# Grouped-query attention: exponentials in place in PSUM, sums divided out early, low parts split on GpSimd

## The chip, the cores and the metric

The kernel runs on one core of one Trainium2 chip. Its time is the device time of one execution in microseconds (us). Five engines work side by side, each through its own instructions in order: TensorE (PE in the profile, with weight loads as PEld), VectorE (DVE), ScalarE (ACT), GpSimd (POOL) and SyncE (SP), which issues most of the DMAs. Matrix products land in PSUM, which has eight banks of 512 fp32 columns; the rest lives in SBUF.

## The reference

Two layers of a trunk with two parallel token mixers. 512 latent tokens and 256 context tokens of width 1024 go through one input projection; branch A is a neighbourhood attention with 8 heads of 64, branch B a grouped-query attention with 8 query heads over 2 key heads, in which latent queries read all 768 keys:

```python
def _attend(q, k, v):
    s = jnp.einsum('bqkgd,btkd->bkgqt', q, k).astype(jnp.float32) * (HEAD_DIM ** -0.5)
    p = jax.nn.softmax(s, axis=-1).astype(v.dtype)
    return jnp.einsum('bkgqt,btkd->bqkgd', p, v)

def _merge(a_att, b_att, a_z, b_z, g_a, g_b, w_o_a, w_o_b, w_out):
    o_a = (a_att * jax.nn.silu(a_z)) @ w_o_a
    o_b = (b_att * jax.nn.silu(b_z)) @ w_o_b
    merged = jax.nn.sigmoid(g_a) * o_a + jax.nn.sigmoid(g_b) * o_b
    return merged @ w_out
```

Context queries read context keys alone, and only layer 0 computes them, since the context of the last layer is not returned. The output is the latent stream.

## The kernel before, in words

Every fp32 product is made of low-precision products: an operand is split into a high part (a cast) and a low part (the operand less its high part), and PE runs high x high, high x low and low x high (`mm3`, L431). Weights are split as they arrive, in `load_w` and `load_w2` (L395, L410): DMA into `raw`, ACT casts to `whi` (L403, L418), and DVE or POOL subtracts to `wlo` (L406, L420). Which of the two is chosen by a small function per load: `pool_lo`, `mix_lo` (every other one on DVE), `bq_lo` (L424 to L426).

A layer goes through five stages: projections for branch A, neighbourhood attention, projections for branch B, grouped-query attention, and the merge with the output projection. Each stage opens its own PSUM tiles (`open_ps`, L103). The bank "f" and the two banks "t" stay open for the whole kernel; a stage adds "s" (scores), "v" (values) or "x" (more accumulators).

The grouped-query stage (L1114 to L1176) runs `pipeline` (L997) over eight heads. For head h it computes the scores, then the values of head h-1, and between them pieces of a list of fill work: gate projections (`g_chunks`, L642) and the first output projection (`o_chunks("a", ...)`, L662), each piece a product over all channels into bank "f", taken out by ACT (L614) or DVE (L692).

One head of 512 latent queries has four blocks of 128 queries by 768 keys (`gq_scores`, L1122). PE writes a block's scores into an "s" tile of two banks (L861, L862); two such tiles exist. DVE finds the row maximum (L1131, which also writes a scratch copy into `p`), ACT writes the exponentials into `p` in SBUF with their sums (L1132), ACT casts them to fp16 `h` (L802), and DVE (blocks 0, 2) or POOL (blocks 1, 3) subtracts for the low part (L803). A transposing DMA on SP's queue turns both parts into `ht` (L804), from which PE makes the values (L1148, L1149). The sums are divided out at the end of a head: `divide` (L806) takes reciprocals, PE spreads each column over partitions by a transpose (L811, four per head and two for its context part), and DVE multiplies them into the gate `zb` (L812). `head_out` (L789) adds the two halves of the value product and multiplies `zb`. In layer 0 each head also has a context part of 2 x 128 queries by 256 keys (`ctx_scores`, `ctx_values`) that goes the same way.

`stage_q` (L849) makes a head's query tile: ACT casts, DVE subtracts (L855). `prepare` (L679) splits the result of branch A, `za`, into `gah` and `gal` (ACT L656, POOL L657) before the first output projection.

The order on each engine isn't that of the text: a scheduler places the instructions when the kernel is built, by its own estimate of durations and of when tiles come free; `behind` pins some to their place. SP's queue, in order, holds weight loads, gate loads and the transposing DMAs together; a weight load waits there until one of three `raw` tiles is free.

Of the kernel before, what the change touches and what calls it, by code (L numbers as in the profile page):

```python
# [27 lines left out]
NP_GQ = (2, 4)  # L28
NH_GQ = (3, 4)
NT_NA = 2  # L30
P_LOG = 9.7
V_UP = 2.0 ** 14
NA_POOL = (1, 3)
SPLIT_POOL = (1, 3)
# [36 lines left out]
def hybrid_kernel(es: ExitStack, tc, x, ctx, cvec, w_ada, w_ada0, small, gvec, w_in, w_o_a, w_o_b, w_out,  # L71
# [28 lines left out]
    ps_pool(es, "t", 2, 512)  # L100
    es.callback(lambda: pm["es"].close())

    def open_ps(x=0, **kinds):  # L103
# [4 lines left out]
        pm["n"], pm["i"], pm["v_for"] = x + 1, 0, ()  # L108
        if x:
            kinds["x"] = (x, 512)  # L110
# [3 lines left out]
    def psw(n=512, kind="w"):  # L114
        if kind == "w":
            kind = "f" if pm["i"] % pm["n"] == 0 else "x"
            pm["i"] += 1
            if pm["i"] in pm["v_for"]:
                kind = "v"
# [464 lines left out]
    def layer(l, hx, nxt, start):  # L584
# [77 lines left out]
        def o_chunks(br, prepare, evac):  # L662
# [96 lines left out]
        if True:  # L759
# [29 lines left out]
            def head_out(po, e, dst, eng=None):  # L789
# [5 lines left out]
                S.copy(a, po[o:o + 64, :n])  # L795
                V.tensor_tensor(a, po[m:m + 64, :n], a, ALU.add)
                (eng or G).tensor_tensor(dst, dst, a, ALU.mult)

            def turned(p, n, out, eng):

                h = att["p"].tile([128, 2, n], F16, tag="h", name=nm("h"), bufs=att["nh"])
                S.copy(h[:, 0], p[:, :n])  # L802
                eng.tensor_tensor(h[:, 1], p[:, :n], h[:, 0], ALU.subtract)  # L803
                nc.sync.dma_start_transpose(out, h.rearrange("p a n -> p (a n)"))  # L804

            def divide(ps, r, e, dst, back):  # L806

                n = r.shape[-1]
                V.reciprocal(r, r)
                for i in range(n):  # L810
                    T.transpose(ps[:, 128 * i:128 * i + 128], r[:, i:i + 1].to_broadcast([128, 128]), ident)  # L811
                V.scalar_tensor_tensor(dst, ps[64 * e:64 * e + 64, :128 * n], back[64 * e:64 * e + 64], dst,  # L812
                                       ALU.mult, ALU.mult)

            def shrink(v, s, mx, row):
# [10 lines left out]
                V.tensor_scalar(s[:, 1:2], s[:, 1:2], 0.5, None, ALU.mult)  # L826
# [22 lines left out]
            def stage_q(src, e):  # L849
# [5 lines left out]
                V.tensor_tensor(rows(qs, 1 - e), q, F(rows(qs, e)), ALU.subtract)  # L855
# [11 lines left out]
            def ctx_scores(q, kh, kl, ct=None):  # L867
# [7 lines left out]
                if ct is not None:  # L875
                    V.tensor_scalar(mx, mx, P_LOG, None, ALU.add)
                p = p_tile()
# [4 lines left out]
                if ct is not None:  # L882
                    turned(p, 512, ct.rearrange("p a i k n -> p (a i k) n"), G)
# [616 lines left out]
```

## Time and profile before

| | |
|---|---|
| median of 3 runs (range) | 1127.67 us (1126.69 to 1128.68) |
| profiled execution | 1127.56 us, its span 1125.6 us |
| mean granted TensorE clock | 0.993 |
| busy PE / PEld / DVE / ACT / POOL | 1093.3 / 905.3 / 774.7 / 579.0 / 490.6 us |
| score blocks of the grouped-query stages | first exponential at 384.5 us, last at 1045.0 us |

Rows of groups name the line, engine, operation, output<-input tiles, shapes and count, then busy time and mean duration, then the engine's idle time before them and what ended it. A row of waits says who waited for whom: total us, times, longest. A row of the timeline begins with start and duration in us. A row of stages gives start and end, length, busy time of each engine with its instruction count, the granted TensorE clock as a share, the DMA share and GB/s. A row of one line's listing gives count and minimum/median/maximum in ns, then first and last start.

### The profile page before, as it was taken

How to read it: one execution, taken by the hardware profiler on the slowest of the kernel's cores; microseconds unless marked ns; L12 is line 12 of the kernel's file. 1: busy time of each engine (PE TensorE's matmuls, PEld its weight loads, DVE VectorE, ACT ScalarE, POOL GpSimd, SP SyncE). 2: the span in 40 equal slices, each digit the busy share in tenths (PEclk: the TensorE clock that was granted, in tenths of full speed). 3: DMA queues.
4: the chain of work that ended last, by engine and by line, in shares of the span. 5: the costliest groups of instructions: out<-in, count | busy, mean ns of one | idle time of the engine just before them, and what ended most of it. 6: DMA issues, size and time to landing. Idle time of an engine off the chain costs nothing.

```text
span 1125.6 us, 16862 instructions
## 1 busy us (share of the span) xinstructions
PE 1093.3 (97%) x5826; PEld 905.3 (80%) x5826; DVE 774.7 (69%) x1492; ACT 579.0 (51%) x1154; POOL 490.6 (44%) x405
## 2 busy tenths in 40 slices
PE   8999999999999999979999999999999999999998
PEld 5688888888998877757788888888888987776677
DVE  4666788897466477776577785458878765677473
ACT  6453266665433576755330284326666446776431
POOL 1054254654247144454521545235554563563531
PEclk9999999999999999989999999999999999999999
DMA  9454322242351488869633532553333236989742
GB/s 373 143 172 140 114 63 66 73 136 89 93 168 38 123 201 185 185 172 269 173 108 125 183 129 72 142 174 92 100 107 116 59 105 172 188 224 239 197 145 80
DMA packets 192222, 161.29 MB, mean 143 GB/s; under 512 B 116364, under 2 KB 158088, under 8 KB 190472
## 3 DMA queue, kind: packets, MB, share of 16 engines
q1 hardware_dynamic: 184800, 145.82, 46.8%
q0 software_dynamic: 2368, 7.87, 2.1%
q10 hardware_dynamic: 4968, 6.53, 1.7%
q8 instruction: 46, 0.75, 0.3%
q14 instruction: 40, 0.33, 0.1%
HBM read 115.58 MB, written 17.32 MB: 118 GB/s over the span
## 4 chain that ended last, share of the span: by engine, by line
PE 38%; issue 4%; DVE 3%; DMA 3%; POOL 2%; ACT 1%; SPq 1%; POOLq 0%; ACTq 0%
PE psx L435 6%; PE psx L433 6%; PE psx L434 6%; PE psf L433 4%; PE psf L434 4%; PE psf L435 4%; PE pss L955 1%; PE pss L861 1%; POOL wlo L406 1%; PE pss L862 1%; PE pst L779 1%; PE pst L1148 1%; DMA raw<-in_w_o_a_dram 1%; PE pst L1149 1%; DMA raw<-in_w_in_dram 1%
## 5 line engine op out<-in xcount | busy, mean ns | idle before, releaser
L420 POOL TENSOR_TENSOR wlo<-raw,whi 128x512 fp32r<-128x512 f32 x70 | 97.9, 1405 | 106.1 <-ACT whi L418 70.4
L433 PE MATMUL psf<-hx,whi 128*128 128x512 f32 (+1 forms) x360 | 138.0, 383 | 3.2 <-ACT zt L614 2.4
L435 PE MATMUL psf<-hx,wlo 128*128 128x512 f32 (+1 forms) x360 | 135.8, 377 | 0.0
L434 PE MATMUL psf<-hx,whi 128*128 128x512 f32 (+1 forms) x360 | 135.1, 375 | 0.0
L433 PE MATMUL psx<-whi,hx 128*128 128x512 f32 (+1 forms) x328 | 120.8, 372 | 0.0
L434 PE MATMUL psx<-wlo,hx 128*128 128x512 f32 (+1 forms) x328 | 119.6, 366 | 0.0
L435 PE MATMUL psx<-whi,hx 128*128 128x512 f32 (+1 forms) x328 | 119.5, 365 | 0.0
L418 ACT CAST whi<-raw 128x512 fp32r<-128x512 f32 x136 | 82.3, 620 | 64.0 <-DMA raw<-in_w_in_dram 35.3
L406 POOL TENSOR_TENSOR wlo<-raw,whi 128x512 fp32r<-128x512 f32 x40 | 61.2, 1535 | 122.1 <-ACT whi L403 80.1
L803 POOL TENSOR_TENSOR h<-p,h 128x768 f16<-128x768 f32 (+1 forms) x40 | 65.7, 1644 | 96.4 <-ACT h L802 72.0
L403 ACT CAST whi<-raw 128x512 fp32r<-128x512 f32 x88 | 54.1, 623 | 99.2 <-PE psx L435 34.2
L420 DVE TENSOR_TENSOR wlo<-raw,whi 128x512 fp32r<-128x512 f32 x66 | 73.6, 1115 | 30.6 <-ACT whi L418 29.0
L504 POOL TENSOR_TENSOR ss<-ss,ehalf 128x8 f32<-128x8 f32 (+2 forms) x40 | 62.5, 1566 | 72.9 <-DVE ss L501 72.8
L433 PEld LDWEIGHTS psf<-hx,whi 128*128 128x128 f32 x360 | 67.9, 188 | 15.4 <-ACT zt L614 3.7
L435 PEld LDWEIGHTS psf<-hx,wlo 128*128 128x128 f32 x360 | 67.8, 188 | 11.6
L1131 DVE CUSTOM_DVE_ANT_0 p<-pss,vb 128x768 f32<-128x768 f32 x64 | 60.3, 953 | 23.6 <-PE pss L862 21.1
L434 PEld LDWEIGHTS psf<-hx,whi 128*128 128x128 f32 x360 | 67.9, 189 | 10.3
L1132 ACT ACTIVATE p<-pss,mx 128x768 f32<-128x768 f32 x64 | 57.6, 900 | 34.7 <-DVE mx L1131 33.7
L435 PEld LDWEIGHTS psx<-whi,hx 128*128 128x128 f32 x328 | 61.9, 189 | 10.0
L434 PEld LDWEIGHTS psx<-wlo,hx 128*128 128x128 f32 x328 | 62.0, 189 | 9.2
L433 PEld LDWEIGHTS psx<-whi,hx 128*128 128x128 f32 x328 | 61.8, 189 | 8.9
L435 PE MATMUL psx<-hx,wlo 128*128 128x256 f32 (+1 forms) x208 | 68.0, 327 | 0.0
(362 smaller groups left out, 3095.8 us busy)
## 6 DMA issues: line engine op xcount, KB each, us to landing
raw<-in_w_in_dram SPq DMA_DIRECT2D x168, 256.0 KB, 2.9
rawb<-in_w_ada_dram SPq DMA_DIRECT2D x48, 256.0 KB, 2.8
raw<-in_w_out_dram SPq DMA_DIRECT2D x32, 256.0 KB, 2.9
tg<-gs SPq DMA_DIRECT2D x4, 1536.0 KB, 6.8
rawx<-in_w_ada_dram SPq DMA_DIRECT2D x4, 1024.0 KB, 9.8
rawy<-in_w_ada_dram SPq DMA_DIRECT2D x4, 1024.0 KB, 9.5
gs<-zt ACTq DMA_DIRECT2D x16, 256.0 KB, 2.0
raw<-in_w_o_a_dram SPq DMA_DIRECT2D x16, 256.0 KB, 3.4
```

The source lines that it names most:

```text
L403: S.copy(hi[:, :n], raw[:, :n])
L406: e.tensor_tensor(lo[:, :n], raw[:, :n], F(hi[:, :n]), ALU.subtract)
L418: S.copy(hi, raw)
L420: lo_eng(i).tensor_tensor(lo, raw, F(hi), ALU.subtract)
L433: T.matmul(ps, lhs[0], rhs[0], start=first, stop=False)
L434: T.matmul(ps, lhs[0], rhs[1], start=False, stop=False)
L435: T.matmul(ps, lhs[1], rhs[0], start=False, stop=last)
L504: G.tensor_tensor(ss, ss, ehalf[:, :n], ALU.pow)
L779: T.transpose(pt[:, c0:c0 + 128], src, ident)
L803: eng.tensor_tensor(h[:, 1], p[:, :n], h[:, 0], ALU.subtract)
L1131: V.tensor_tensor_reduce(p, pss, lift, -1.0, 3e38, ALU.add, ALU.min, mx[:, 0:1])
L1132: S.activation(p, pss, AF.Exp, bias=mx[:, 0:1], accum_out=r[:, i:i + 1])
```

## The change

It rewrites the grouped-query stage and what feeds it, in both layers.

- The tiles "s" become two of three banks (1536 columns). `gq_scores` takes two blocks at a time: one row maximum over both, then two exponentials written over the scores, in PSUM. The SBUF tiles `p` are gone there, and with them the constant `P_LOG`.
- `turned` divides first: per block a reciprocal of the sum and a scaling by 2^14 (one column each, DVE), then ACT's cast from PSUM with that scale, then on DVE one instruction that scales and subtracts. POOL no longer takes part. `divide` is removed; `head_out` takes the scale back with the values' own factor.
- The context part of layer 0 does the same, and is put behind the fill work (`rest` in `values_of`).
- "t" is opened per stage: two banks as before, but one in the grouped-query stage, where "v" is gone.
- Low parts that move to POOL: those of all gate weights (`g_chunks`), of the weights of the first output projection, and of the grouped-query queries.

```diff
-NP_GQ = (2, 4)
-NH_GQ = (3, 4)
+NH_GQ = (5, 6)
-P_LOG = 9.7
+P_UP = 2.0 ** 14
...
-    ps_pool(es, "t", 2, 512)
-    def open_ps(x=0, **kinds):
+    def open_ps(x=0, t=2, **kinds):
...
+        kinds["t"] = (t, 512)
...
-            return fill_chunks(col0, None, gs[c], False, mix_lo)
+            return fill_chunks(col0, None, gs[c], False, pool_lo)
...
-                    st["w"] = load_w2(src, 256 * i, 4, pool_lo if br == "b" and i == 0 else mix_lo)
+                    st["w"] = load_w2(src, 256 * i, 4, pool_lo if br == "a" or i == 0 else mix_lo)
...
-                S.copy(a, po[o:o + 64, :n])
-                V.tensor_tensor(a, po[m:m + 64, :n], a, ALU.add)
+                if back is None:
+                    S.copy(a, po[o:o + 64, :n])
+                    V.tensor_tensor(a, po[m:m + 64, :n], a, ALU.add)
+                else:
+                    S.activation(a, po[o:o + 64, :n], AF.Copy, scale=back[o:o + 64])
+                    V.scalar_tensor_tensor(a, po[m:m + 64, :n], back[m:m + 64], a, ALU.mult, ALU.add)
                 (eng or G).tensor_tensor(dst, dst, a, ALU.mult)
...
-            def turned(p, n, out, eng):
+            def turned(p, r, cuts, out):
+                n = cuts[-1][1]
                 h = att["p"].tile([128, 2, n], F16, tag="h", name=nm("h"), bufs=att["nh"])
-                S.copy(h[:, 0], p[:, :n])
-                eng.tensor_tensor(h[:, 1], p[:, :n], h[:, 0], ALU.subtract)
+                for i, (c0, c1) in enumerate(cuts):
+                    V.reciprocal(r[:, i:i + 1], r[:, i:i + 1])
+                    V.tensor_scalar(r[:, i:i + 1], r[:, i:i + 1], P_UP, None, ALU.mult)
+                    S.activation(h[:, 0, c0:c1], p[:, c0:c1], AF.Copy, scale=r[:, i:i + 1])
+                    V.scalar_tensor_tensor(h[:, 1, c0:c1], p[:, c0:c1], r[:, i:i + 1], h[:, 0, c0:c1],
+                                           ALU.mult, ALU.subtract)
                 nc.sync.dma_start_transpose(out, h.rearrange("p a n -> p (a n)"))
...
-                V.tensor_tensor(rows(qs, 1 - e), q, F(rows(qs, e)), ALU.subtract)
+                eng.tensor_tensor(rows(qs, 1 - e), q, F(rows(qs, e)), ALU.subtract)
...
-                if ct is not None:
-                    V.tensor_scalar(mx, mx, P_LOG, None, ALU.add)
-                p = p_tile()
+                p = p_tile() if ct is None else pss
...
-                    ps = psw(512, "v")
-                    po = ps[:, 0:256]
-                    divide(ps[:, 256:512], r, e, dst, back)
+                    po = psw(256, "t")
...
-            gq_es = open_att(f"gq{l}", 768, NP_GQ[l], NH_GQ[l])
-            open_ps(s=(2, 1024), v=(1, 512))
+            gq_es = open_att(f"gq{l}", 768, 0, NH_GQ[l])
+            open_ps(t=1, s=(2, 1536))
...
-                for i in range(4):
-                    pss = ps_score(768)
-                    scores(pss, q[:, 128 * i:128 * i + 128], kh, kl,
+                for j in range(2):
+                    ps = ps_score(1536)
+                    scores(ps, q[:, 256 * j:256 * j + 128], kh, kl,
                            [(0, 512, cut(0, 512)), (512, 256, cut(512, 768))])
-                    p = p_tile()
+                    scores(ps, q[:, 256 * j + 128:256 * j + 256], kh, kl,
+                           [(768, 256, cut(0, 256)), (1024, 512, cut(256, 768))])
                     mx = sp.tile([128, 2], F32, tag="mx", name=nm("mx"), bufs=8)
-                    V.tensor_tensor_reduce(p, pss, lift, -1.0, 3e38, ALU.add, ALU.min, mx[:, 0:1])
-                    S.activation(p, pss, AF.Exp, bias=mx[:, 0:1], accum_out=r[:, i:i + 1])
-                    turned(p, 768, ht[:, i], G if i in SPLIT_POOL else V)
-                    run(att["bg"], 1)
-                return ht, r
+                    V.tensor_reduce(mx, ps.rearrange("p (i n) -> p i n", i=2), AX, ALU.max, negate=True)
+                    r = sp.tile([128, 2], F32, tag="r", name=nm("r"), bufs=8)
+                    for i in range(2):
+                        p = ps[:, 768 * i:768 * i + 768]
+                        S.activation(p, p, AF.Exp, bias=mx[:, i:i + 1], accum_out=r[:, i:i + 1])
+                    for i in range(2):
+                        turned(ps[:, 768 * i:768 * i + 768], r[:, i:i + 1], [(0, 768)], ht[:, 2 * j + i])
+                        run(att["bg"], 1)
+                return ht
...
-                divide(psw(512, "t"), r, e, dst, vs[:, 1:2])
...
-                q = stage_q(qbv[:, h // 2, :], h % 2)
+                q = stage_q(qbv[:, h // 2, :], h % 2, G)
```

More of the change, by code (lines that the diff above doesn't have):

```diff
@@ L787, in transpose_split, with head_out @@
                 return hi, lo
-            def head_out(po, e, dst, eng=None):
+            def head_out(po, e, dst, eng=None, back=None):
                 n = dst.shape[-1]
@@ L825, in shrink @@
                 V.reciprocal(s[:, 0:1], s[:, 1:2])
-                V.tensor_scalar(s[:, 1:2], s[:, 1:2], 0.5, None, ALU.mult)
+                V.tensor_scalar(s[:, 1:2], s[:, 1:2], 0.5 / P_UP, None, ALU.mult)
             def rows(a, half):
```

53 lines of the change are left out of this document (23 added, 30 removed).

## The prediction

> **What bounds the kernel now.** I read the page's busy shares first, then stages chosen by what runs in them, then waits, then time around the worst wait. In this table of stages each row gives the stretch, its length, and for PE, PEld, DVE, ACT and POOL the busy time.
>
> ```profile
> span 1125.6 us, 16862 instructions
> PE 1093.3 (97%) x5826; PEld 905.3 (80%) x5826; DVE 774.7 (69%) x1492; ACT 579.0 (51%) x1154; POOL 490.6 (44%) x405
> 0.00:380.00 380.00, 375.96 (x2161) 318.33 (x2162) 260.46 (x573) 192.91 (x406) 157.31 (x142) 1.00 0.39 127
> 380.00:580.00 200.00, 184.81 (x1030) 149.70 (x1029) 136.01 (x237) 112.72 (x218) 87.38 (x62) 0.97 0.75 185
> 580.00:935.00 355.00, 352.98 (x1793) 297.44 (x1793) 259.64 (x500) 172.68 (x354) 165.43 (x150) 1.00 0.38 117
> 935.00:1075.00 140.00, 134.86 (x630) 102.34 (x629) 92.79 (x146) 92.02 (x164) 68.62 (x47) 1.00 0.87 205
> ```
>
> PE sets the time nearly everywhere: outside the two grouped-query stages it idles 4.0 us before 380 and 2.0 us between 580 and 935. The stages that the change rewrites, 380 to 580 (layer 0) and 935 to 1075 (layer 1), hold 15.2 + 5.1 = 20.3 us of PE idle, so both PE work and PE waits are worth time there. The next rows are PE's waits in 380 to 560, then the execution around the longest, then busy time and granted clock (third figure from the end) in 5 us pieces.
>
> ```profile
> PE psv L811 <- DVE ho L796: 5.8, 1, 5.8
> ...
> PE pss L861 <- ACT p L880: 1.3, 1, 1.3
> PE pss L861 <- ACT p L1132: 0.9, 1, 0.9
> 491.54 7.15 POOL L657 TENSOR_TENSOR gal<-za,gah 128x768 fp32r<-128x768 f32 x4
> 492.20 8.26 DVE L420 TENSOR_TENSOR wlo<-raw,whi 128x512 fp32r<-128x512 f32 x1
> 501.67 0.42 DVE L796 TENSOR_TENSOR ho<-psv,ho 64x256 f32<-64x256 f32 x1
> 490.00:495.00 5.00, 2.78 (x12) 1.94 (x11) 4.94 (x5) 4.88 (x12) 5.00 (x4) 0.82 0.93 369
> 495.00:500.00 5.00, 1.35 (x5) 0.86 (x3) 5.00 (x1) 1.83 (x4) 4.91 (x4) 0.84 1.05 314
> 500.00:505.00 5.00, 2.85 (x9) 2.47 (x10) 4.06 (x7) 0.00 (x0) 1.85 (x2) 0.50 0.11 25
> 505.00:510.00 5.00, 5.00 (x21) 3.11 (x21) 2.40 (x5) 1.83 (x3) 1.65 (x1) 0.82 0.85 183
> ```
>
> One DVE subtraction of weights (L420) lasts 8.26 us, from just after four POOL subtractions begin until the POOL work there ends. Behind it stands the head's output addition (L796), and PE waits 5.8 us for that. PE then runs at a lowered clock: busy time times the missing clock is 0.5 + 0.2 + 1.4 + 0.9 = 3.0 us. This one wait costs 8.8 us.
>
> **The change part by part.** The rows that follow carry its prices: from listings by line (minimum/median/maximum in ns), one piece of the chain, and groups by shape (busy, mean | idle before it).
>
> ```profile
> L811 PE MATMUL pst<-ident,r x64: 270/272/323, 395.6 to 1050.1; 128*128 128x128 f32 x64
> L811 PE MATMUL psv<-ident,r x16: 270/272/476, 399.6 to 540.8; 128*128 128x128 f32 x16
> 954.69 0.44 PE pst L811 x4
> L420 DVE TENSOR_TENSOR wlo<-raw,whi x66: 666/694/8258, 97.4 to 1053.8; 128x512 fp32r<-128x512 f32 x66
> L420 POOL TENSOR_TENSOR wlo<-raw,whi x70: 1263/1297/2012, 93.7 to 1054.6; 128x512 fp32r<-128x512 f32 x70
> L692 DVE SCALAR_TENSOR_TENSOR tg<-tg,psf x24: 416/682/690, 507.3 to 1050.0; 128x512 f32<-128x512 f32 x16, 128x256 f32<-128x256 f32 x8
> L826 DVE TENSOR_SCALAR vb<-vb x2: 154/154/154, 342.5 to 915.5; 128x1 f32<-128x1 f32 x2
> L876 DVE TENSOR_SCALAR mx<-mx x8: 133/297/1416, 395.8 to 535.8; 128x2 f32<-128x2 f32 x8
> L855 DVE TENSOR_TENSOR qs<-qb,qs x16: 685/860/1209, 371.1 to 1017.3; 64x768 fp32r<-64x768 f32 x8, 64x512 fp32r<-64x512 f32 x8
> L845 POOL TENSOR_TENSOR gk<-kb,gk x4: 1850/2030/2203, 339.8 to 914.8; 64x768 fp32r<-64x768 f32 x4
> L1131 DVE CUSTOM_DVE_ANT_0 p<-pss,vb 128x768 f32<-128x768 f32 x64 | 60.3, 953 | 23.6 <-PE pss L862 21.1 <-POOL h L803 1.8
> L1132 ACT ACTIVATE p<-pss,mx 128x768 f32<-128x768 f32 x64 | 57.6, 900 | 34.7 <-DVE mx L1131 33.7 <-ACT zt L614 0.8
> L803 DVE TENSOR_TENSOR h<-p,h 128x768 f16<-128x768 f32 x32 | 35.5, 1110 | 22.5 <-ACT h L802 22.1
> L803 POOL TENSOR_TENSOR h<-p,h 128x768 f16<-128x768 f32 x32 | 56.0, 1750 | 89.7 <-ACT h L802 70.1 <-issue 13.8 <-PE psf L435 5.1
> L802 ACT CAST h<-p 128x768 f16<-128x768 f32 x64 | 52.6, 831 | 5.5 <-DMA ht<-h 2.5 <-DMA ct<-h 2.3
> L874 DVE TENSOR_REDUCE mx<-pss 128x2 f32<-128x512 f32 x16 | 11.0, 686 | 3.4 <-PE pss L862 3.3
> ```
>
> 1. *Transposes of the sums go* (`divide`). Four take 0.44 us of PE, so 16 heads give 16 x 0.44 = 7.0 us and the eight context pairs 8 x 0.22 = 1.8 us: 8.8 us less PE work, on the path as long as PE is busy. DVE loses the two products per head with them, off the path.
>
> 2. *Weights' low parts move from DVE to POOL*: ten gate pieces and four of the first output projection in each of these stages (14 x 1.30 = 18 us more POOL), and six gate pieces earlier in each layer, which POOL's idle hides. The DVE instruction of 8.26 us is among them, so the 8.8 us above go. POOL also loses its share of the splits: 16 x 1.75 = 28 us in each stage and the eight context splits.
>
> 3. *The queries' low parts move to POOL*: eight a layer, 0.86 us in the middle on DVE, about 2 us on POOL (L845 has the same shape), staged in the built order about a head ahead of use, which hides them. Only the first head of layer 1 has no cover: up to 1 us, taken as 0.5.
>
> 4. *The split of the probabilities* reads PSUM on DVE for all 64 blocks, and two tiny instructions per block (reciprocal, scaling) come in. DVE's sum per two blocks is before 2 x 0.95 + 1.11 = 3.0 us, after a reduction over 1536, two splits of 0.96 and four of 0.16. The reduction I estimate from 0.69 us at 512 and 0.95 at 768: 1.06 ns an element, 1.77 us. That is 4.3 us, so 1.3 us more for each of 32 pairs; the moved work (28 x 0.69 + 16 x 0.86 = 33 us) and the products of `divide` take about as much off DVE again. ACT keeps its instruction counts. Writing exponentials into PSUM has no row; a copy into SBUF of 768 takes 0.83 and the exponential 0.90, so I take 0.90, with 0.1 us either way (3 us on 32 pairs if all of it showed).
>
> Would POOL hold the new tiny DVE instructions up? The scaling of two columns (L876) reached 1.4 us, each long one ending with a POOL instruction; the scaling of one column (L826) took 0.154 us both times, while POOL was busy with L845. The new ones have one column, so I take 0.16. The Trainium skill, "SBUF — State Buffer", section "Who interferes with whom", lets any `tensor_scalar` into the two-port modes that lock against GpSimd; by it the new ones would pay L876's median excess of about 0.15 us, 80 x 0.15 = 12 us of DVE in all. The two L826 rows speak against it.
>
> 5. *Score tiles are held longer.* Now a tile of one block frees after L1131 and L1132. After, a tile has two blocks, 1536 columns on three PSUM banks, and frees after the last split. The built order makes ACT's copy of the second block wait for DVE's split of the first, as they share the middle bank. The chain is 1.77 + 2 x 0.98 + 0.74 + 0.96 + 0.74 + 0.96 = 7.1 us (exponentials 0.98 and copies 0.74 apart, from these starts):
>
> ```profile
> 483.29 0.90 ACT L1132 ACTIVATE p<-pss,mx 128x768 f32<-128x768 f32 x1 [0.52 <-DVE mx L1131]
> 484.31 0.83 ACT L802 CAST h<-p 128x768 f16<-128x768 f32 x1
> 485.05 0.90 ACT L1132 ACTIVATE p<-pss,mx 128x768 f32<-128x768 f32 x1
> ```
>
> There are six hand-overs. Idle before L1131 and L1132 is 23.6/64 = 0.37 and 34.7/64 = 0.54 us; at 0.45 each the hold is 9.8 us. The Trainium skill, "PSUM — Partial Sum Buffer", section "PSUM bank collisions raise a hardware error", says that two engines may not touch one bank at once; no run here can show that, and the wait in the order is what it would ask for.
>
> In the built PE order, work between the last use of a tile and the next use of its buffer is 8 to 12 us in most places (5.6 once), counted at the 0.22 to 0.23 us of a 512-column matmul (the last row below, a piece of the chain; the row above it is the landing time of the probabilities' turning DMAs). A hold of 9.8 us with the scatter of any wait takes some 0.35 us at each of 29 uses whose predecessor is a full tile: 10 us, less the present 3.6 us (0.9 and 1.3 above, 1.4 in layer 1): +6.5 us. With a hold at the bare 7.1 us it is -3.6 (the present waits go); at 12 us it is about +30.
>
> ```profile
> PE pss L861 <- ACT p L1132: 1.4, 3, 0.8
> PEld psf L433 <- DVE tg L692: 5.4, 12, 0.9
> DMA to landing us min/median/max: 3.0/4.2/11.7
> 950.11 0.23 PE psf L434
> ```
>
> 6. *One bank for values instead of three.* With one "t" bank and one "f" bank, PE's fill pieces stand back to back more often: by my count of the two orders there are 12 places with 0.5 us or less of other work between, and 7 now. Each costs 5.4/12 = 0.45 us: +2.3 us (0 to 6). The last head of layer 1 has 10.4 us of PE work between its last scores and its values; hold 7.1 plus 4.2 us of landing is 11.3: +1 us.
>
> *The sum*: -8.8 - 8.8 + 0.5 + 6.5 + 2.3 + 1.0 = -7.3 us. The profiled execution took 1127.56 us (span 1125.6), 0.1 us from the median 1127.67, so I forecast 1120.3 us.
>
> **The rivals.**
> A. *PE stays full.* For it: PE's other idle is small, and DVE no longer meets POOL's locks: L692, with one operand in PSUM, never passes 0.69 us, while L420 does. Then points 5 and 6 cost nothing and the present tile waits go: 1127.6 - 17.6 - 3.6 = 1106 us.
> B. *The stall moves to POOL.* POOL still does the four subtractions of 7.15 us, now with weights and queries behind them in its queue. If PE waits for one of these as long as it did for L796, the 8.8 us stay: 1120.3 + 8.8 = 1129 us. Against: weights are split one piece ahead, and PE's piece lasts 2.6 us or more.
> C. *Score tiles become the bound* (the other side). Place: the second halves of both stages, where pieces of PE work are short and ACT and DVE alternate on one tile. At a hold of 12 us, about what the chain comes to where other ACT work stands between its steps, PE loses some 30 us: 1120.3 + 23.5 = 1144 us. It decides from a hold of about 10.5 us, where new tile waits eat the 7 us that are left. For it: ACT's order puts weight casts and gate evacuations between two exponentials of one tile. Against: the present two buffers cost only 3.6 us.
> D. *Gains and new waits cancel*: within 0.2% (2.3 us, about what a measurement of this kernel can tell from no change), 1127 us.
>
> **How the numbers follow.** Forecast (1108 to 1125): 0.42. A: 0.12. B: 0.12, half within 0.2%, half above. C: 0.26. D: 0.08. Faster is 0.42 + 0.12 = 0.54, same 0.08 + 0.06 = 0.14, slower 0.26 + 0.06 = 0.32. The forecast's own range is 1110 to 1125; the range for all runs from 1103, a little below A, to 1146, just past C.
>
> **What would show it.** Right: no `divide` rows; PE at about 1093.3 - 8.8 - 3.0 = 1082 us busy; no DVE weight subtraction of 8 us and no clock of 0.5 near 500; PE waits on the splits' release of score tiles of about 10 us in sum. C shows as waits of PE's score matmuls for DVE's split of 20 us or more, with lowered clock if single waits pass some 5 us. B shows as PE waiting for POOL's `wlo`, `gal` or `qs`. Wrong for another reason would be exponentials into PSUM well off 0.9 us, the one-column scalings well over 0.16 us, or time lost outside 380 to 580 and 935 to 1075, where the "t" banks now move from stage to stage.

## The result and the profile after

The changed kernel takes 1135.23 us in the median of four runs (1133.83 to 1138.47), the kernel before, run beside it, 1127.69 (1126.69 to 1128.68): ratio 1.0071, 95% interval 1.0047 to 1.0095. It is 0.7% slower, where 1120.3 us, faster, was forecast. The profiled execution took 1138.47 us, the slowest of the four, at a mean clock of 0.986 (0.991 to 0.995 in the other three), so sums of the trace overstate the loss by some 3 us.

The page of the changed kernel, then its stages as in the prediction (stretch, length, busy time of PE, PEld, DVE, ACT, POOL, granted clock, DMA share, GB/s). Lines moved: scores are L859 and L860 here, the row maximum L1127, exponentials L1131, reciprocal and scaling L806 and L807, ACT's copy and DVE's split of the probabilities L808 and L809, values L1145 and L1146, queries' low parts L853, weights' high and low parts L416 and L418, the fill pieces' ways out L612 and L690, the gated values' split L654 and L655.

```profile
span 1136.7 us, 16695 instructions
...
PE 1094.3 (96%) x5746; PEld 899.9 (79%) x5746; DVE 751.9 (66%) x1490; ACT 588.4 (52%) x1162; POOL 487.0 (43%) x421
```

```profile
380.00:580.00 200.00, 186.31 (x1008) 148.68 (x1007) 134.57 (x274) 121.36 (x233) 73.96 (x57) 0.97 0.79 191
580.00:935.00 355.00, 351.76 (x1780) 295.55 (x1780) 246.00 (x475) 168.69 (x346) 174.85 (x160) 1.00 0.38 114
935.00:1075.00 140.00, 122.68 (x532) 89.34 (x532) 81.72 (x131) 90.90 (x155) 57.16 (x45) 0.95 0.84 192
0.00:380.00 380.00, 376.15 (x2155) 318.04 (x2156) 253.81 (x559) 193.02 (x406) 170.40 (x154) 1.00 0.40 127
```

The third row holds the loss: in layer 1's grouped-query stage PE idles 17.3 us (5.1 before), and its clock is 0.95 (1.00 before), another 6.1 us of busy time. No single wait makes it. PE's waits in that stage, then four pieces of it in which the clock fell:

```profile
PE pss L859 <- POOL qs L853: 4.1, 2, 2.1
PE pst L1145 <- DMA ht<-h: 3.3, 2, 2.1
PE psf L431 <- ACT zt L612: 2.3, 2, 1.7
PE pss L859 <- DVE r L806: 2.0, 2, 1.8
PE psx L431 <- DVE h L809: 1.7, 1, 1.7
PE pss L859 <- DVE h L809: 1.7, 2, 1.2
```

```profile
940.00:945.00 5.00, 5.00 (x22) 4.22 (x22) 3.47 (x3) 1.66 (x4) 0.96 (x1) 0.77 0.04 16
980.00:985.00 5.00, 5.00 (x17) 2.92 (x16) 0.81 (x2) 1.73 (x4) 0.18 (x1) 0.68 0.44 89
1010.00:1015.00 5.00, 5.00 (x18) 3.84 (x17) 3.66 (x4) 3.62 (x7) 4.92 (x5) 0.66 1.02 366
1030.00:1035.00 5.00, 5.00 (x18) 4.00 (x19) 3.54 (x7) 3.35 (x7) 1.20 (x1) 0.66 1.04 211
```

Queries late on POOL, turned probabilities late, score tiles not free, the fill bank not emptied: about 2 us at a time, under four names. Each of these four pieces follows a wait of 1.8 to 2.1 us (twice for queries, once each for turned probabilities and a score tile) and loses 1.2 to 1.7 us more to the clock.

The new instructions themselves came out nearly as priced, by listings of a line (minimum/median/maximum in ns) and by groups (busy, mean):

```profile
L807 DVE TENSOR_SCALAR r<-r x80: 133/154/156, 389.1 to 1064.1; 128x1 f32<-128x1 f32 x80
...
L1127 DVE TENSOR_REDUCE mx<-pss x32: 1739/1756/1758, 385.6 to 1058.1; 128x2 f32<-128x1536 f32 x32
...
L853 POOL TENSOR_TENSOR qs<-qb,qs x16: 1255/1542/1848, 372.6 to 1028.6; 64x768 fp32r<-64x768 f32 x8, 64x512 fp32r<-64x512 f32 x8
...
L418 DVE TENSOR_TENSOR wlo<-raw,whi x26: 672/693/1770, 97.7 to 1059.8; 128x512 fp32r<-128x512 f32 x26
```

```profile
L809 DVE SCALAR_TENSOR_TENSOR h<-pss,r,h 128x768 f16<-128x768 f32 x64 | 64.6, 1015 | 31.6 <-ACT h L808 31.1
...
L1131 ACT ACTIVATE pss<-pss,mx 128x768 f32<-128x768 f32 x64 | 55.8, 872 | 29.4 <-DVE mx L1127 28.8
```

### The profile page after: what moved, and what is told of

Its sections match the earlier page's. It is cut to its first block, busy times and chain, and to the rows that moved or that the text cites. A ratio compares the mean times of both kernels' runs of the same rounds, so it can differ in the third digit from the quotient of the medians.

```text
span 1136.7 us, 16695 instructions
## 1 busy us (share of the span) xinstructions
PE 1094.3 (96%) x5746; PEld 899.9 (79%) x5746; DVE 751.9 (66%) x1490; ACT 588.4 (52%) x1162; POOL 487.0 (43%) x421
## 4 chain that ended last, share of the span: by engine, by line
PE 70%; issue 7%; DVE 7%; ACT 6%; DMA 5%; POOL 4%; SPq 1%; POOLq 0%; ACTq 0%; DVEq 0%
PE psx L431 10%; PE psx L433 10%; PE psx L432 10%; PE psf L431 7%; PE psf L432 7%; PE psf L433 7%; PE pss L859 2%; PE pst L777 2%; PE pss L860 2%; PE pss L948 2%; ACT pss L1131 2%; DMA raw<-in_w_in_dram 2%; ACT h L808 1%; DVE h L809 1%; POOL wlo L418 1%
## 5 line engine op out<-in xcount | busy, mean ns | idle before, releaser
L418 POOL TENSOR_TENSOR wlo<-raw,whi 128x512 fp32r<-128x512 f32 x110 | 146.1, 1340 | 137.5 <-ACT whi L416 91.0
L431 PE MATMUL psf<-hx,whi 128*128 128x512 f32 (+1 forms) x360 | 139.4, 387 | 7.7 <-ACT zt L612 6.9
L432 PE MATMUL psf<-hx,whi 128*128 128x512 f32 (+1 forms) x360 | 136.5, 379 | 0.0
L416 ACT CAST whi<-raw 128x512 fp32r<-128x512 f32 x136 | 82.9, 620 | 74.2 <-DMA raw<-in_w_in_dram 45.5
L404 POOL TENSOR_TENSOR wlo<-raw,whi 128x512 fp32r<-128x512 f32 x40 | 56.3, 1408 | 137.7 <-ACT whi L401 98.1
L809 DVE SCALAR_TENSOR_TENSOR h<-pss,r,h 128x768 f16<-128x768 f32 (+1 forms) x80 | 72.1, 908 | 33.8 <-ACT h L808 33.3
L1127 DVE TENSOR_REDUCE mx<-pss 128x2 f32<-128x1536 f32 x32 | 55.8, 1754 | 40.2 <-PE pss L860 40.1
L808 ACT ACTIVATE h<-pss,r 128x768 f16<-128x768 f32 (+1 forms) x80 | 63.8, 813 | 14.8 <-DVE h L809 12.0
L1131 ACT ACTIVATE pss<-pss,mx 128x768 f32<-128x768 f32 x64 | 55.8, 872 | 29.4 <-DVE mx L1127 28.8
L431 PE MATMUL psx<-hx,whi 128*128 128x256 f32 (+1 forms) x208 | 68.2, 328 | 0.0
```

The source lines that it names most:

```text
L404: e.tensor_tensor(lo[:, :n], raw[:, :n], F(hi[:, :n]), ALU.subtract)
L416: S.copy(hi, raw)
L418: lo_eng(i).tensor_tensor(lo, raw, F(hi), ALU.subtract)
L431: T.matmul(ps, lhs[0], rhs[0], start=first, stop=False)
L432: T.matmul(ps, lhs[0], rhs[1], start=False, stop=False)
L808: S.activation(h[:, 0, c0:c1], p[:, c0:c1], AF.Copy, scale=r[:, i:i + 1])
```

## The experiments

Seventeen runs. The table gives the median, the ratio to the kernel before with its interval, and four stretches of the profiled execution: to layer 0's first grouped-query scores; from there to the first transposition of layer 1's window probabilities; to layer 1's first grouped-query scores; to the end. "Pairs" are two-block score tiles, "ones" one-block tiles.

| kernel | us | ratio (95%) | to S0 | to N1 | to S1 | to end |
|---|---|---|---|---|---|---|
| before | 1127.7 | 1 | 382.6 | 398.2 | 157.4 | 187.4 |
| changed | 1135.2 | 1.0071 (1.0047, 1.0095) | 384.0 | 393.8 | 160.8 | 198.1 |
| e1 changed, queries on DVE | 1142.7 | 1.0135 (1.0115, 1.0155) | 384.5 | 396.2 | 161.5 | 198.7 |
| e2 changed, weights shared | 1129.6 | 1.0025 (1.0014, 1.0036) | 382.7 | 387.5 | 156.6 | 200.6 |
| e3 changed, ones | 1131.3 | 1.0037 (1.0021, 1.0052) | 383.5 | 396.2 | 158.8 | 190.9 |
| e4 before, weights on POOL | 1133.2 | 1.0063 (1.0048, 1.0078) | 386.4 | 397.0 | 159.5 | 188.0 |
| e5 before, queries on POOL | 1122.1 | 0.9964 (0.9951, 0.9976) | 381.4 | 393.9 | 157.3 | 187.8 |
| e6 ones, weights shared | 1130.4 | 1.0040 (1.0024, 1.0055) | 382.3 | 399.2 | 161.4 | 185.3 |
| e7 e2 with the transposes | 1131.6 | 1.0046 (1.0033, 1.0059) | 382.5 | 392.5 | 157.0 | 195.6 |
| e8 changed, gates' weights shared | 1136.9 | 1.0097 (1.0081, 1.0113) | 381.2 | 391.9 | 159.0 | 202.9 |
| e9 changed, ones in layer 1 | 1127.7 | 1.0006 (0.9997, 1.0014) | 384.0 | 390.1 | 159.5 | 192.1 |
| e10 e9, weights shared | 1114.1 | 0.9885 (0.9872, 0.9898) | 382.4 | 387.6 | 156.6 | 184.6 |
| e11 before, 24 transposes | 1130.9 | 1.0037 (1.0024, 1.0049) | 382.8 | 404.3 | 159.0 | 184.5 |
| e12 changed, projection's weights shared | 1132.3 | 1.0042 (1.0026, 1.0059) | 383.9 | 387.5 | 158.7 | 200.4 |
| e13 e10 with the transposes | 1121.5 | 0.9949 (0.9934, 0.9965) | 383.0 | 393.5 | 157.0 | 185.7 |
| e14 e10, queries on DVE | 1137.2 | 1.0098 (1.0081, 1.0115) | 381.3 | 400.2 | 159.8 | 193.8 |
| e15 e10, context values early | 1114.8 | 0.9891 (0.9877, 0.9906) | 382.3 | 388.5 | 156.6 | 185.2 |
| e16 e10, gates' weights on POOL | 1118.9 | 0.9927 (0.9913, 0.9940) | 383.7 | 387.6 | 158.9 | 186.6 |
| e17 e10, queries twice | 1140.8 | 1.0123 (1.0104, 1.0141) | 382.3 | 402.7 | 160.2 | 193.8 |

The scheduler places every edited kernel anew, on all engines, so each price includes that. Two pairs are free of it ahead of layer 1's scores: up to 920 us the instructions of every engine stand in the same order in the changed kernel and e9, and in e2 and e10, so these differ in layer 1 alone. Stretches are of one execution and carry some 2 to 4 us of scatter: the changed kernel and e9 still differ by 3.7 us in the second.

**Queries back on DVE (e1), weights shared again (e2).** In the changed kernel:

```diff
# e1
-                q = stage_q(qbv[:, h // 2, :], h % 2, G)
+                q = stage_q(qbv[:, h // 2, :], h % 2, V)
# e2
-            return fill_chunks(col0, None, gs[c], False, pool_lo)
+            return fill_chunks(col0, None, gs[c], False, mix_lo)
-                    st["w"] = load_w2(src, 256 * i, 4, pool_lo if br == "a" or i == 0 else mix_lo)
+                    st["w"] = load_w2(src, 256 * i, 4, pool_lo if br == "b" and i == 0 else mix_lo)
```

> The changed kernel with one line undone: the low parts of the grouped-query queries are subtracted on DVE again, as before. Theory Q (queries late on GpSimd): in the changed kernel's trace PE waits 2.07 us at 936.6 and 2.03 us at 1027.8 for qs of POOL, and each wait is followed by about 1.5 us lost to a lowered clock; with DVE doing it both go: 1135.2 - 7 = about 1128 us. Theory T (the two-block score tiles and the chain of hand-overs on ACT and DVE are the bound): DVE gets 16 subtractions of 0.69 to 0.86 us into that chain and the waits only change their names: 1134 to 1138 us.

> The changed kernel with the weights' low parts of the gates and of the first output projection shared between DVE and POOL again, as before. Theory of the prediction's point 2 (removing the 8.26 us DVE subtraction was worth 8.8 us): one of them meets the four POOL subtractions near 490 again, so it gets slower by up to 8.8 us: 1140 to 1144 us, with a DVE subtraction of about 8 us in the trace. Rival: the stall only showed where DVE was needed just then; with POOL emptier the queries come earlier: 1130 to 1135 us.

Both theories of e1 fell: 7.5 us slower, not faster or equal. The two waits for POOL's `qs` are gone with e1, one of 1.4 us for DVE's is there instead, and others grow past them: in 380 to 580 PE waits 9.5 us for ACT to empty the fill bank, 4.6 in the changed kernel. e2 gained 5.7 us, against the prediction's point 2: the weights on POOL were a cost, not a gain. Nor did the stall come back: the longest DVE weight subtraction of e2's trace lasts 2.88 us.

**Weights on POOL alone (e4).** The same two lines, in the kernel before.

> The kernel before with one part of the change alone: the low parts of the gates' weights and of the first output projection go to POOL. The prediction's point 2: the 8.26 us DVE subtraction and PE's 5.8 us wait with its lowered clock go: 1127.7 - 8.8 = 1119 us. Rival: the same place stalls on POOL instead, since its queue now holds the weights behind the four subtractions of 7.15 us, or behind the 1.75 us splits that POOL still does here: 1126 to 1132 us.

6.2 us slower, above the rival's range. The stall only changed its victim. In e4's trace, the listing of the splits `h` in layer 0's stage, then POOL's and DVE's instructions around 500:

```profile
L803 DVE TENSOR_TENSOR h<-p,h x16: 940/959/6647, 391.4 to 531.7; 128x768 f16<-128x768 f32 x16
```

```profile
495.87 5.43 POOL L657 TENSOR_TENSOR gal<-za,gah 128x768 fp32r<-128x768 f32 x3
501.27 1.14 POOL L803 TENSOR_TENSOR h<-p,h 128x512 f16<-128x512 f32 x1
502.38 3.69 POOL L420 TENSOR_TENSOR wlo<-raw,whi 128x512 fp32r<-128x512 f32 x3
...
500.24 6.65 DVE L803 TENSOR_TENSOR h<-p,h 128x768 f16<-128x768 f32 x1 [0.16 <-ACT h L802]
```

A split that takes 0.96 us lasts 6.65 and ends 0.8 us after the last of the weights, which now make POOL's run longer. PE waits 6.5 us at 508.6 for the DVE instruction that is to empty the fill bank; the wait that the prediction wanted to remove was 5.8 us long. Elsewhere a DVE instruction of the modulation (L295, 0.7 us otherwise) lasts 6.44 us at 256.8 behind weights on POOL, and PE waits 2.3 us: the stretches ahead of the grouped-query stages lose 3.8 and 2.1 us.

**One-block tiles in both layers (e3), with the weights shared (e6).** Three tiles of two banks in place of two of three:

```diff
-            open_ps(t=1, s=(2, 1536))
+            open_ps(t=1, s=(3, 1024))
...
+                for i in range(4):
+                    ps = ps_score(768)
+                    scores(ps, q[:, 128 * i:128 * i + 128], kh, kl,
+                           [(0, 512, cut(0, 512)), (512, 256, cut(512, 768))])
+                    V.tensor_reduce(mx[:, 0:1], ps, AX, ALU.max, negate=True)
+                    S.activation(ps, ps, AF.Exp, bias=mx[:, 0:1], accum_out=r[:, 0:1])
+                    late.append((ps, r[:, 0:1], [(0, 768)], ht[:, i]))
+                    if i:
+                        turned(*late.pop(0))
```

> The changed kernel with score tiles of one block: three tiles of two banks in place of two tiles of three banks; each block has its own reduction over 768, and its split stands behind the exponential of the next block. Nothing else differs; the banks for values and fills stay one each. Theory T: hold of a tile falls from about 8 us for two blocks to about 5 for one, no block waits for the other's bank, and most of the idle in 935 to 1075 (17.3 us) goes: 1122 to 1129 us. Theory Q: the waits on qs stay, only the small score waits go: 1132 to 1136 us. Theory B (the single banks for values and fills): no change, 1134 to 1137 us.

> The changed kernel with both edits that made it faster: score tiles of one block, and the weights' low parts shared between DVE and POOL. If their causes are apart (POOL's queue ahead of the rotations and in the earlier stages; the hold of a two-block tile), the gains add: 1135.2 - 3.9 - 5.7 = 1125.6 us. If both gave PE the same idle back (DVE late in the second grouped-query stage), the second adds little or DVE's added 30 us cost the gain: 1129 to 1132 us.

The medians, 3.9 us and no addition, hide two opposite effects: the last stretch falls from 198.1 and 200.6 us to 190.9 and 185.3, while layer 0's grows from 387.5 (e2) to 399.2 (e6). In e6 PE waits there 12.3 us for ACT to empty the fill bank, in e2 4.9.

**One-block tiles in layer 1 alone (e9), with the weights shared (e10).** `if not first:` ahead of e3's loop, `s=(2, 1536) if first else (3, 1024)`; e10 adds e2's lines.

> The changed kernel with score tiles of one block in layer 1 alone; layer 0 keeps its two-block tiles, and everything else is as changed. In the traces so far the end of layer 1, from its first grouped-query scores, takes 198 us with two-block tiles and 191 with one-block tiles (187 before), while a tile of two blocks is held 11.8 us there and the next head comes after 14 to 15 us. Theory T1 (the two-block tile is what slows layer 1, since hold and scores fill the whole time of a head): 1135.2 - 7 = 1128 us, or down to 1124. If layer 0 is where one-block tiles helped: 1134 to 1136 us.

> As the run before, and the weights' low parts shared between DVE and POOL as in the kernel before. Theory T1 with the costs of the weights on POOL apart from it: stages summed from the traces, 382.7 + 387.5 + 98.1 up to layer 1's rotations (two-block tiles, weights shared), 59 to 63 to its first scores, 185 to 191 after them (one-block tiles) = 1113 to 1122 of span, 1114 to 1124 us, faster than both kernels. If the two gains are one and the same idle, as in the run with one-block tiles in both layers and shared weights: 1129 to 1131 us.

Both as the first theory has them: 7.6 us gained by e9, and e10 at 1114.1 us is 1.15% faster than the kernel before. A tile's hold, from the end of its last scores to the end of its last split, is 10.5 us in the mean in layer 0 of the changed kernel and 11.8 (up to 13.8) in layer 1; one-block tiles are held 7.1 us there. With a pair's scores (1.6 us from 975.1) a tile is taken for 13 to 14 us, and a head, from values to values, lasts 15.5 on average (108.2 us for seven), so PE can hardly run ahead. In layer 0 of the same kernel a tile is taken for some 12 us, and a head lasts 19.9; in layer 1 of e10 a head lasts 13.7. What stretches the hold shows around one wait of the changed kernel (rows of ACT, DVE and PE):

```profile
1003.60 0.87 ACT L1131 ACTIVATE pss<-pss,mx 128x768 f32<-128x768 f32 x1
1004.39 0.19 ACT L1131 ACTIVATION_READ_ACCUMULATOR pss<-pss,mx 128x1 f32 x1
1004.49 2.17 ACT L654 CAST gah<-za 128x512 fp32r<-128x512 f32 x4
1006.56 0.62 ACT L416 CAST whi<-raw 128x512 fp32r<-128x512 f32 x1
1007.08 0.89 ACT L808 ACTIVATE h<-pss,r 128x768 f16<-128x768 f32 x1
...
1008.01 1.02 DVE L809 SCALAR_TENSOR_TENSOR h<-pss,r,h 128x768 f16<-128x768 f32 x1 [3.04 <-ACT h L808]
1008.94 0.15 DVE L806 RECIPROCAL r<-r 128x1 f32<-128x1 f32 x1
...
1009.17 0.47 PE L859 MATMUL pss<-gk,qs 128*128 128x512 f32 x1 [1.83 <-DVE r L806]
```

An exponential of the other tile, four casts of the gated values and a weight cast stand in ACT's order ahead of the copy that the split needs. DVE idles 3.04 us for it, and PE 1.83. (The view names the reciprocal; the split, which ends at 1009.03, is what frees the tile.) In e10 the stage looks like this, its stretches shifted to its own times, and its waits from 926 to 1070:

```profile
380.00:580.00 200.00, 186.39 (x1044) 149.90 (x1043) 147.61 (x294) 123.63 (x238) 62.17 (x46) 1.00 0.83 199
580.00:920.00 340.00, 338.17 (x1713) 284.54 (x1712) 244.44 (x474) 165.79 (x339) 159.25 (x148) 1.00 0.37 112
920.00:1060.00 140.00, 133.44 (x614) 100.92 (x613) 99.60 (x171) 95.45 (x165) 51.66 (x39) 1.00 0.89 207
```

```profile
PE pss L859 <- DVE h L809: 2.5, 3, 1.6
PE psf L431 <- DVE tg L690: 1.6, 2, 0.8
```

PE idles 6.6 us in 140, at full clock; the rows are its two largest waits, and no wait on the queries is left in that stretch, though they still come from POOL. The four kernels form a square: pairs or ones in layer 1, weights on POOL or shared: 1135.2, 1127.7, 1129.6, 1114.1. Each step is worth 5.7 or 7.6 us alone and 13.5 or 15.4 after the other, so each cost hid part of the other. From e2 to e10, where layer 1 alone differs, the last stretch falls by 16.0 us and the three others stay within 0.3.

**Which weights (e8, e12, e16).** One of e2's two lines at a time, in the changed kernel (e8 gates, e12 projection); e16 is e10 with the gates on POOL.

> The changed kernel with the low parts of the gates' weights shared between DVE and POOL as before; those of the first output projection stay on POOL. If POOL's added work in the stages ahead of the grouped queries is what costs (gate pieces between the window stage's heads and between the rotations of the queries; the projection's weights are only loaded inside the grouped-query stages), this gets all of the gain: 1129 to 1131 us. If the four subtractions of the gated values with the projection's weights behind them are the place: 1134 to 1136 us.

> The changed kernel with the weights' low parts of the first output projection shared between DVE and POOL as before; those of the gates stay on POOL. With the gates shared instead the time did not fall (1136.9 us), with both shared it fell by 5.7. If the projection's weights on POOL, behind the four subtractions of the gated values, are the cost: 1128 to 1130 us. If only both together cost (POOL's queue as a whole): 1133 to 1136 us.

> The kernel of 1114.1 us with the gates' weights' low parts on POOL as in the change; the first output projection's stay shared between DVE and POOL. All weights on POOL cost 13.5 us here (1127.65 us). If the gates are the larger part (POOL's queue ahead of the window stage's work, of the rotations and of layer 1's first queries; a DVE instruction of 4.2 us at 231 behind a run of POOL work): 1119 to 1124 us. If the projection's weights behind the four subtractions of the gated values are: 1115 to 1118 us.

Inconclusive in the changed kernel: the gates alone give nothing (+1.7), the projection alone 2.9 of 5.7. In e10's kernel the gates cost 4.8 us, so the projection's weights account for the other 8.8 of 13.5. The stretches of e16 against e10 put the gates' part ahead of the grouped-query stages (to S0 +1.3, to S1 +2.3) and into the last stretch (+2.0): there layer 1's first scores wait 2.1 us for POOL's queries, as in the changed kernel and e9, and not in e2 or e10. Ahead of layer 0's scores, with gates on POOL, a DVE instruction is held at 231 by a run of POOL work, in the changed kernel as in e12 and e16, and not in e2, e8 or e10; POOL's rows of the changed kernel, then DVE's:

```profile
231.31 2.52 POOL L418 TENSOR_TENSOR wlo<-raw,whi 128x512 fp32r<-128x512 f32 x2
233.79 1.03 POOL L766 TENSOR_TENSOR p<-p,r 128x512 f32<-128x512 f32 x1
...
231.17 4.20 DVE L293 CUSTOM_DVE_ANT_0 rawb<-rawb,cb 128x512 f32<-128x512 f32 x1
```

**Queries on POOL (e5, e14, e17).** e5 gives the kernel before the change's `stage_q` alone; e14 gives e10 e1's line; e17 keeps e10's and adds the same subtraction on DVE, into a tile nobody reads:

```diff
                 eng.tensor_tensor(rows(qs, 1 - e), q, F(rows(qs, e)), ALU.subtract)
+                if eng is G:
+                    qx = att["p"].tile([128, n], BF16, tag="qx", name=nm("qx"), bufs=1)
+                    V.tensor_tensor(rows(qx, 1 - e), q, F(rows(qs, e)), ALU.subtract)
```

> The kernel before with one part of the change alone: the low parts of the grouped-query queries are subtracted on POOL. The prediction's point 3: +0.5 us (the first head of layer 1), so 1127.5 us. Theory D (DVE stands between ACT and PE in these stages, so that each DVE subtraction taken away there is worth time; it is what made the changed kernel 7.5 us slower when the queries came back to DVE): 12 us of DVE work leave, 1120 to 1125 us. Theory Q (POOL has a queue of its own, with splits of 1.75 us and the four subtractions of 7.15 us ahead of the queries): 1130 us or more, with PE waiting for qs of POOL.

> The kernel of 1114.1 us with the grouped-query queries' low parts on DVE again. Theory D (DVE stands between ACT and PE, so its 12 us of subtractions are on the path in part): 4 to 8 us more, 1118 to 1122 us, as in the kernel before, where moving them to POOL gave 4.9, and in the changed kernel, where moving them back cost 7.5. The prediction's point 3 (DVE off the path): 1113.6 us.

> The kernel of 1114.1 us, whose queries' low parts stay on POOL, with the same 16 subtractions made a second time on DVE into a scratch tile that nothing reads. Moving them to DVE cost 23 us. If the cost is DVE's time and its waiting there for ACT's cast (8.5 us of idle in 16 waits, with reductions and splits queued behind), it comes back without any reader: 1126 to 1137 us. If the cost is that PE's scores then wait for DVE's queue to reach the queries, it stays away: 1114 to 1118 us.

e5 is 4.9 us faster than the kernel before, e14 23.1 us slower than e10, e17 26.7. So PE waiting for queries in DVE's queue is not what costs: the loss comes back in e17, where nobody reads what DVE makes, and from 370 to 1080 no wait of PE in e14 or e17 names queries of DVE. It is DVE's time in these stages, or the new placement that comes with it. PE's wait that grows most, from 380 to 580, is for ACT to empty the fill bank; e10's row, then e14's (10.5 us in e17):

```profile
PE psf L431 <- ACT zt L612: 4.5, 4, 1.9
PE psf L431 <- ACT zt L612: 10.2, 7, 3.4
```

The rows of e14, then of e17, from 380 to 1075 (busy, mean | idle before):

```profile
L853 DVE TENSOR_TENSOR qs<-qb,qs 64x768 fp32r<-64x768 f32 x6 | 6.3, 1050 | 0.3 <-ACT qs L852 0.2
...
L853 DVE TENSOR_TENSOR qs<-qb,qs 64x512 fp32r<-64x512 f32 x8 | 6.1, 763 | 1.2 <-ACT qs L852 0.9
```

```profile
L856 DVE TENSOR_TENSOR qx<-qb,qs 64x768 bf16<-64x768 f32 x6 | 11.0, 1831 | 0.4 <-ACT qs L852 0.2
...
L856 DVE TENSOR_TENSOR qx<-qb,qs 64x512 bf16<-64x512 f32 x8 | 9.7, 1218 | 1.3 <-ACT qs L852 0.9
```

DVE hardly waits for ACT's casts (1.5 us in e14; the 8.5 us of the expectation counted the window stage too). 12.4 us of DVE work cost 23.1 in e14, though DVE is busy 213.3 of 290 us in e10's two stages; e17's second subtraction is dearer, 20.7 us, and so no equal measure. How much of the excess is the new placement stays open; e15, placed anew too, moved by 0.7.

**Transposes (e7, e11, e13).** e7 and e13 put 80 transposes back into e2 and e10; e11 takes 56 of them from the kernel before: it leaves out the division of all blocks of a head but the first, which are divided by the first block's sums.

```diff
# e7, e13
+                for i in range(4):
+                    T.transpose(po[:, 128 * i:128 * i + 128], ident, ident)
# e11, in divide
-                for i in range(n):
-                    T.transpose(ps[:, 128 * i:128 * i + 128], r[:, i:i + 1].to_broadcast([128, 128]), ident)
+                T.transpose(ps[:, 0:128], r[:, 0:1].to_broadcast([128, 128]), ident)
```

> The changed kernel with the weights shared as before, and the 80 transposes put back on PE: four ahead of each head's values and two ahead of each context pair, of the identity, into the bank that the values then overwrite. The prediction's point 1: 8.8 us of PE work on the path, so 1129.6 + 8.8 = 1138 us. Rival: in these stages PE has 13.6 and 18.8 us of idle, and the transposes stand where PE would wait anyway: 1130 to 1133 us.

> The kernel before with 56 of the 80 transposes of the sums left out: only the first block's sums are transposed, and all blocks of a head are divided by them (the division of the other blocks is left out of the computation). The prediction's point 1 (PE work on the path): 56 x 0.11 = 6.2 us off 1127, 1120.8 us. Rival, from the transposes put back into the changed kernel at 2.0 us for 8.8 us of work: PE waits instead for what was to come next, and no more than 1.5 us goes: 1125.5 to 1127 us.

> The kernel of 1114.1 us (two-block tiles in layer 0, one-block tiles in layer 1, weights shared) with the 80 transposes put back on PE, of the identity, into the bank that the values overwrite. Where the two-block tiles held layer 1 up, 8.8 us of transposes cost 2.0. If that was because PE stood idle there anyway, they cost more here, where layer 1's idle is 6.2 us and no longer 18.8: about 2.5 in layer 0 and 3.5 in layer 1, 1120 us. If the prediction's point 1 holds outright: 1123 us. If waits cover them here too: 1116 us.

The same transposes cost 2.0 us in e2, where pairs keep PE waiting in layer 1, and 7.4 in e10, where they don't. In e11 the last stretch falls by 2.9 us, about the 24 x 0.11 = 2.6 of its transposes there, while layer 0 gets 6.1 us longer: there the scaling of a maximum, 0.3 us in the middle in the kernel before, lasts 7.06 us at 494.8 under POOL's run, and PE waits 4.5 us at 504.8 for what DVE owes behind it. Neither theory foresaw that.

**Late context values (e15).** e10 with `rest()` called at once, ahead of the fill.

> The kernel of 1114.1 us with the context values of layer 0 put straight behind the head's values again, ahead of the fill pieces, as in the kernel before. The prediction gave this part no cost and no gain: 1113 to 1115 us. If the one bank that values now have makes two value products in a row wait for its evacuation (ACT 0.68 and DVE 0.73 us with their hand-overs, 1.5 to 2 us at each of eight places), it is up to 15 us slower: 1118 to 1129 us.

0.7 us slower, within what these runs tell: no cost or gain of this part shows.

## Why the prediction was wrong

Point by point.

1. *Transposes, -8.8*: the work was sized right, its place on the path only with the tiles out of the way (7.4 us in e13); in the changed kernel with shared weights it was 2.0. PE's busy time did not fall to the forecast 1082 us but stayed at 1094.3: busy time times missing clock, summed over pieces of 5 us, went from 4.4 to 14.2 us and filled what the 80 transposes left.

2. *Weights to POOL, -8.8*: this step failed, in sign. Alone it costs 6.2 us (e4), in the changed kernel 5.7 (e2), with one-block tiles in layer 1 13.5 (e10). "POOL's idle hides them" was wrong for the gate pieces (4.8 us in e16), and the stall was not tied to the weight: a split, a modulation step or a scaling of two columns takes its place (6.65, 6.44 and 7.06 us in e4 and e11). In the changed kernel it is absent with the weights shared too (e2), so their move is not what removed it; that DVE's splits now read PSUM, and are never held, would explain it, but no run shows that alone.

3. *Queries to POOL, +0.5*: the first head's wait was seen rightly, but it is 2.07 us with a lowered clock behind it, and a later head waits 2.03. The larger error is the other side: DVE's subtractions were counted as off the path, and their leaving is worth 4.9 to 23 us.

4. *DVE's and ACT's prices*: right for the reduction (1.77 estimated, 1.756), the exponential (0.90, 0.872) and the scaling (0.16, 0.154). The Trainium skill, "SBUF — State Buffer", "Who interferes with whom", would have let the scalings lock against POOL "when their operands meet the conditions" of the two-port modes, a condition that the prediction left out; none of the 80 of one column passed 0.156 us, though one of two columns was held in e11. Its rule there, that a DVE instruction with two SBUF inputs contends and one with at most one, outside the two-port modes, does not, fits the rows: `h<-pss,r,h` never passed 1.02 us, while the split from SBUF, the weight subtraction and the modulation did. Split and copy (0.90 us) were 0.06 and 0.07 us dearer than taken.

5. *Tiles held longer, +6.5*: the hold was taken as 9.8 us and measured 10.5 and 11.8. The wait did not show on the tiles, 3.7 us in layer 1, but under many names, with the clock behind. The sum had no term for a lowered clock behind new waits, and the signs expected one only behind waits of some 5 us; waits of 1.8 to 2.1 us brought it, and of the busy time in the profiled execution 14.2 us went to it, against 4.4 before and 1.3 in e10. In layer 1 alone the pairs cost 7.6 us, or 15.4 with shared weights; in layer 0 they are better than one-block tiles by 3.7 (e3 and e9) to 16.3 us (e6 and e10). Rival C named this mechanism: its 1144 us stand for a hold of 12 us in both layers, where only layer 1 comes near that hold and pays.

6. *One bank for values, +2.3, last head, +1.0*: not tried alone.

Without point 2 the prediction's sum is +1.5 us; e2, the change without its weights, measured 2.5 us. That agreement is luck: points 1, 3 and 5 were each off by more, in both directions. Rival B's price, 1129 us, lay 6 us under the measured time. One of the two late queries does stand behind a weight in POOL's queue (1.27 us from 1027.23), but the stall that B named did not come: PE waits at most 0.5 us at a time for `gal`.

Still open: how much of the pairs' cost in layer 1 is the hold itself and how much that the probabilities of two blocks reach the turning DMA later, since one-block tiles change both.

## What to carry to other kernels

Work removed from the busiest engine is worth its time only where no hand-over chain is tighter than that engine: here 8.8 us of PE work was worth 2.0 or 7.4, by the kernel around it. Before work is moved to an "idle" engine, look at which instructions of other engines run beside it, and count the longest unbroken run that it makes there. Size a tile so that its hold plus its refill stays well below the time between two uses, in each layer by that layer's period; and try the parts of a change apart, since two harmful parts can hide each other. A wait of 2 us on PE can cost nearly twice its length: in these traces up to 3.41 us at half clock, 1.7 us of work, came behind it.

## What the hardware showed unexpectedly

Short waits cost clock, but not always: waits of 1.8 to 2.1 us in the changed kernel were followed by pieces at 0.66 to 0.77, while in e1 waits of 2.45 us from 999.5 and 1.82 us from 1009.2 were not. e1's pieces:

```profile
1000.00:1005.00 5.00, 3.07 (x15) 2.43 (x16) 4.41 (x9) 4.26 (x8) 1.28 (x1) 1.00 0.78 153
1010.00:1015.00 5.00, 3.99 (x19) 3.40 (x20) 3.40 (x5) 4.03 (x8) 5.00 (x5) 1.00 0.93 314
```

The traces show why equal waits differ. In each of them the stretches at half clock begin on one grid of 3.41 us and last one to three of its steps, so what counts is PE's idle time within a step. The wait for queries in the changed kernel lies in one step, and the next is at half clock; e1's longer wait is shared by two steps, 1.40 and 1.05 us, and nothing follows:

```profile
935.46:938.87 3.41, 1.34 (x6) 0.80 (x6) 0.00 (x0) 2.90 (x6) 2.75 (x3) 1.00 0.71 229
938.87:942.28 3.41, 3.41 (x12) 2.82 (x12) 0.85 (x1) 0.00 (x0) 1.06 (x1) 0.50 0.35 131
```

```profile
997.46:1000.87 3.41, 2.02 (x10) 0.78 (x7) 3.35 (x4) 2.20 (x4) 0.00 (x0) 1.00 0.51 115
1000.87:1004.29 3.42, 2.36 (x12) 1.85 (x13) 2.89 (x7) 3.31 (x7) 0.66 (x1) 1.00 0.61 117
```

Eighteen of the nineteen profiled executions have half-clock steps between 100 us and 20 us before the end (e10 has none). In them, a step at full clock with less than 1.75 us of PE idle was never followed by one at half clock, and a step with more than 1.9 us always was, save one of 2.02 us in e11. In between both happened: 1.83 us in the changed kernel (1009.17) brought a drop, e1's 1.82 us did not. The Trainium skill, "TensorE: Matmul & The Clock Gate", Part 1, puts the drop after an idle window of about 3.4 us and calls the window free-running; the second fits the grid, and the first asks for more idle time than was needed here. The runs of one kernel spread with the clock: e3's twelve spans go from 1124.2 us at a clock of 0.996 to 1134.2 at 0.988.

Nor is DVE held each time it meets POOL: in e10's trace the four subtractions of the gated values run from 479.1, and a weight subtraction that starts on DVE under them takes 1.16 us, where the same pair took 8.26 us in the kernel before.

```profile
479.09 7.65 POOL L655 TENSOR_TENSOR gal<-za,gah 128x768 fp32r<-128x768 f32 x4
...
480.33 1.16 DVE L418 TENSOR_TENSOR wlo<-raw,whi 128x512 fp32r<-128x512 f32 x1 [3.09 <-ACT whi L416]
```
